# A matmul with GELU: the third product of the opening, evacuated partial sums, a load by row halves and a moved GELU

## Chip, cores, metric

One core of one Trainium2 chip. The metric is the device time of one execution in microseconds (us), the median of several runs.

## The reference

```python
x = np.matmul(a, b)          # a, b: 4096 x 4096 float32
return 0.5 * x * (1 + np.tanh(np.sqrt(2 / np.pi) * (x + 0.044715 * x**3)))
```

## The kernel before

The kernel cuts A, B and the output into quadrants (11, 12, 21, 22) and uses a seven-product scheme (M1 to M7) on them, for 16 groups of 512 rows by 512 columns of each quadrant. Two chains of PSUM banks, X and Y (four banks each, one for each block of 128 rows), take the products. VectorE makes the sums and differences of operands (aS, bS), transposes A and combines results; ScalarE copies PSUM to SBUF and computes GELU; GpSimd issues the loads, which cast f32 to f16.

Group 0 is special, because its operands are still being loaded: the first half of its contraction is done as eight plain products (`PLAIN`), and only the second half by M3, M5, M7, M1, M4, M2, M6, in this order. One step is half a product: 16 matmuls. The parts that matter:

```python
PLAIN = [   # quadrant of C, of A, of B, by row halves
    ("12", "11", "12", False), ("11", "11", "11", False), ("12", "12", "22", False), ("11", "12", "21", False),
    ("21", "21", "11", True), ("21", "22", "21", True), ("22", "21", "12", True), ("22", "22", "22", True),
]
N_WARM = 44
N_IDLE = 10
...
# in settle(), after the last step of a product, for each row block i
elif name == "M7" and not end:
    post["x7", i] = keep("x7", X, RT)          # ScalarE copy, RT = 4 buffers named x7
...
elif name == "M2":
    y = new_y()                                # 5 buffers named y
    tt(y, post.pop(("x1", i)), Y, ALU.subtract)   # VectorE reads bank Y; M6 writes it next
    ...
    waiting.append((gi, i, 1, 0, y, y))
elif name == "M6":
    y = new_y()
    tt(y, Y, post.pop(("x7", i)), ALU.add)
    flush()                                    # adds what is in post, then GELU and output
    ...
...
for n, whats in (      # what is issued ahead of step n; _0 and _1: first and second half
    (0, "A11_0 B12_0 T11_0 B11_0 A12_0 B22_0 B21_0 A21_0"),
    (4, "T12_0 A22_0"), (7, "T21_0"),
    (8, "A11_1+B12_1+B22_1 T22_0 A12_1+B21_1"),
    (14, "T11_1 A22_1 B11_1"), (16, "T12_1 A21_1"), (18, "S2 S3 T22_1"), (22, "T21_1"),
): ...
...
for n, step in enumerate(steps):
    for fn, args in before.get(n, ()):
        fn(*args)
    if n + AHEAD < len(steps):                 # sums are made two steps ahead
        make_sums(*steps[n + AHEAD])           # (cut)
    flush()
    combine()
    plain(n) if step[1] < 0 else multiply(*step)
```

`A` and `B` are loads, `T` is VectorE's transpose of an A block, `S2` and `S3` make M7's B sums ahead of time, `+` mixes loads with one another. Instructions of an engine run in the order in which they are issued here.

Of the kernel before, what the change touches and what calls it, by code (L numbers as in the profile page):

```python
# [8 lines left out]
F16 = mybir.dt.float16  # L9
# [4 lines left out]
ALU = mybir.AluOpType  # L14
AX = mybir.AxisListType

P = 128
Q = 32
NC = 512
# [3 lines left out]
RT = 4  # L23
TM = RT * P
AHEAD = 2
# [16 lines left out]
QPH = 4  # L42
# [1 line left out]


PLAIN = [
    ("12", "11", "12", False), ("11", "11", "11", False), ("12", "12", "22", False), ("11", "12", "21", False),
    ("21", "21", "11", True), ("21", "22", "21", True), ("22", "21", "12", True), ("22", "22", "22", True),
]
N_PLAIN = 2 * len(PLAIN)  # L50
N_WARM = 44
N_IDLE = 10


SQUARE_MAX = 2.0**26
# [45 lines left out]
def half_path(  # L101
# [9 lines left out]
    nc = tc.nc  # L111
    M, K = a.shape
    _, N = b.shape
# [5 lines left out]
    pool = ctx.enter_context(tc.tile_pool(name="sb", bufs=1))  # L119
# [13 lines left out]
    a_tiles, b_tiles = {}, {}  # L133
# [54 lines left out]
    def part(tiles, blk, quad, q):  # L188

        t = tiles[blk, quad, q // 2].rearrange("p x y -> p (x y)")  # L190
        w = 4 * NC
        return t[:, (q % 2) * w : (q % 2 + 1) * w]
# [83 lines left out]
    sums = {}  # L276

    def product(gi, s):
        return (LAST if gi == len(groups) - 1 else PRODUCTS)[s]

    def make_sums(gi, s, q, only=None):
        mb, nb = groups[gi]
        _, _, oa, ob = product(gi, s)
        got = []
        for tiles, blk, o, tag in ((a_tiles, mb, oa, "aS"), (b_tiles, nb, ob, "bS")):
            if only not in (None, tag):
                continue
            if isinstance(o, str):
                got.append(part(tiles, blk, o, q))
                continue  # L290
            if (tag, gi, s, q) in sums:
                got.append(sums.pop((tag, gi, s, q)))
                continue
            t = pool.tile([P, 4 * NC], F16, name=tag, tag=tag, bufs=AHEAD + 1)
            nc.vector.tensor_tensor(  # L295
                out=t[:, :], in0=part(tiles, blk, o[0], q), in1=part(tiles, blk, o[1], q),
                op=ALU.add if o[2] > 0 else ALU.subtract,
            )
            got.append(t)
            if tag == only:  # L300
                sums[tag, gi, s, q] = t
                return
        sums[gi, s, q] = got
# [7 lines left out]
    banks = {}  # L311
    post = {}

    def bank(gi, chain, i):
        par = (gi + (chain == "Y")) % 2
        t = psum_pool.tile([P, NC], F32, name=f"acc{chain}", tag=f"bank{par}{i}")
        banks[chain, i] = t
        return t
# [11 lines left out]
    def warm():  # L330
        z = pool.tile([P, NC], F16, name="zeros", tag="bS", bufs=AHEAD + 1)
        nc.vector.memset(z[:, :], 0.0)
        w = pool.tile([P, P], F16, name="none", tag="none")
        nc.vector.memset(w[:, :], 0.0)
        post["none"] = w
        for i in range(RT):
            bank(0, "X", i)
            bank(0, "Y", i)
        for _ in range(N_WARM):
            nc.tensor.matmul(  # L340
                banks["X", RT - 1][:, :], z[:, :P], z[:, :], start=True, stop=True, skip_group_check=True
            )

    def idle(n):

        for _ in range(n):
            nc.tensor.matmul(
                banks["X", 0][:, :], post["none"][:, :], b_tiles[0, "12", 0][:, 0, :],
                start=False, stop=False, skip_group_check=True,
            )  # L350

    def plain(n):

        (quad, oa, ob, by_rows), h = PLAIN[n // 2], n % 2
        chain = "X" if quad == "11" else "Y"
        seen = [x for x in range(len(PLAIN)) if PLAIN[x][0] == quad]
        sa, sb = a_tiles[0, oa, 0], b_tiles[0, ob, 0]
        sa = sa.rearrange("p jj (m e) -> p jj m e", e=2)
        tiles = [(j, e) for j in range(NJ // 2) for e in range(2) if by_rows or e == h]
        for i in range(h * RT // 2, (h + 1) * RT // 2) if by_rows else range(RT):  # L360
            acc = banks[chain, i]
            start = n // 2 == seen[0] and (by_rows or h == 0)
            stop = n // 2 == seen[-1] and (by_rows or h == 1)
            for j, e in tiles:
                nc.tensor.matmul(
                    acc[:, :], sa[:, j, i * P : (i + 1) * P, e], sb[:, 2 * j + e, :],
                    start=start and (j, e) == tiles[0], stop=stop and (j, e) == tiles[-1],
                    skip_group_check=True,
                )
            if not stop:  # L370
                continue
            if quad == "12":
                post["c12", i] = keep("x7", acc, RT)
            elif quad == "11":
                tt(post["c12", i], post["c12", i], acc, ALU.add)
            elif quad == "21":
                tag = ("energy1", "energy2", "square", "square")[i]
                t = pool.tile([P, W], BF16, name="c21", tag=tag, bufs=1 + (i > 1)).bitcast(F32)
                nc.scalar.copy(out=t[:, :], in_=acc[:, :])
                post["c21", i] = t  # L380
            else:
                tt(post["c12", i], post["c12", i], acc, ALU.subtract)

    def multiply(gi, s, q):
        name, chain = product(gi, s)[:2]
        first = q == 0 and name in ("M3", "M5")
        sa, sb = sums.pop((gi, s, q))
        for i in range(RT):
            acc = bank(gi, chain, i) if first else banks[chain, i]
            products(acc, sa, sb, i, first, q == QPH - 1)  # L390
            if q == QPH - 1:
                settle(gi, name, i)

    def keep(tag, src, bufs):
        t = pool.tile([P, NC], F32, name=tag, tag=tag, bufs=bufs)
        nc.scalar.copy(out=t[:, :], in_=src[:, :])  # L396
        return t
# [3 lines left out]
    def flush():  # L401

        for args in waiting:
            gi, i, ih, jh, y, _ = args
            plain_part = post.pop((f"c{ih + 1}{jh + 1}", i), None) if gi == 0 else None
            if plain_part is not None:
                tt(y, y, plain_part, ALU.add)
            emit(*args)
        waiting.clear()
# [21 lines left out]
    def tt(o, x, y, op):  # L431
        nc.vector.tensor_tensor(out=o[:, :], in0=x[:, :], in1=y[:, :], op=op)  # L432
# [44 lines left out]
    before = {}  # L477
# [5 lines left out]


    for n, whats in (
        (0, "A11_0 B12_0 T11_0 B11_0 A12_0 B22_0 B21_0 A21_0"),
        (4, "T12_0 A22_0"),
        (7, "T21_0"),
        (8, "A11_1+B12_1+B22_1 T22_0 A12_1+B21_1"),
        (14, "T11_1 A22_1 B11_1"),  # L490
        (16, "T12_1 A21_1"),
        (18, "S2 S3 T22_1"),
        (22, "T21_1"),
    ):
        for what in whats.split():
            half = what[-1] == "0" and what != "A11_0"
            if what[0] == "S":
                before.setdefault(n, []).append((make_sums, (0, 2, int(what[1]), "bS")))
                continue
            for h in (0, 1) if half else (None,):  # L500
                args = [(x[0], (0, x[1:3], int(x[4]), h)) for x in what.split("+")]
                if what[0] == "T":
                    before.setdefault(n, []).append((turn_a, args[0][1]))
                else:
                    pairs = [({"A": load_a, "B": load_b}[x], xs) for x, xs in args]
                    before.setdefault(n, []).append((load, pairs))
    before[4].append((idle, (N_IDLE,)))


    nxt_b = {"12": "22", "22": "21", "21": "12", "11": "11"}  # L510
# [33 lines left out]
    for mb in range(NMB):  # L544
        for which, gi in (("b", mb * NNB + 1), ("a", mb * NNB + 2)):
            blk = groups[gi][which == "b"]
# [5 lines left out]
            for x, piece in enumerate(pieces):  # L552
                n = max(x // 2, x - n_two)
# [21 lines left out]
    with tc.manual_schedule():  # L575
        warm()
        table = pool.tile([P, 1], F32, name="table", tag="table")
        nc.vector.memset(table[:, :], 0.0)
        nc.scalar.activation(table[:, :], table[:, :], ACT.Gelu_apprx_tanh)
# [3 lines that stand above are left out]
            if n + AHEAD < len(steps):  # L583
                gi, s, q = steps[n + AHEAD]
                if s >= 0:
                    make_sums(gi, s, q)
            flush()
            combine()
            if step[1] < 0:
                plain(n)  # L590
            else:
                multiply(*step)
        flush()
    return said["value"]

# [35 lines left out]
```

## Time and profile before

| | before |
|---|---|
| time, first three runs | 1581.33 us (1580.16 to 1581.53) |
| span in the profile | 1578.4 us |
| TensorE busy | 99% |
| idle of TensorE after the first real matmul | 2.1 us (0.16, 1.79 and 0.19), and 2.15 us of idle matmuls |

TensorE hardly waits. The real work is 7200 matmuls of 0.216 us; everything in question is in the first 130 us. The prediction shows the lines.

### The profile page before, as it was taken

What the parts mean: (1) busy time and instruction counts of PE and PEld (TensorE: products, weight loads), DVE (VectorE), ACT (ScalarE), POOL (GpSimd) and SP (SyncE); (2) the same over time, 40 slices, a digit from 0 to 9 for tenths busy, and PEclk for the clock granted to TensorE, in tenths of its full rate; (3) what the DMA queues carried; (4) which work ended last, traced back from release to release, by engine and by line L of the source; (5) the groups of instructions that cost most, each with busy time, mean ns of one, the idle gap of its engine ahead of it and who ended that gap; (6) DMA issues with size and microseconds to landing.
All of it is one profiled execution on the core that took longest, in us unless ns stands there. A gap on an engine that the chain in (4) does not pass through costs nothing. (4 is left out here: it accounts for less than half of the span.)

```text
span 1578.4 us, 19668 instructions
## 1 busy us (share of the span) xinstructions
PE 1568.0 (99%) x7254; PEld 710.0 (45%) x7254; DVE 1228.0 (78%) x1371; ACT 517.8 (33%) x710; POOL 537.4 (34%) x976
## 2 busy tenths in 40 slices
PE   9999999999999999999999999999999999999998
PEld 4444444444444444444444444444444444444443
DVE  1498888967787888895778788887687778988775
ACT  0026445311122545531111344542211145364111
POOL 7763442430234144341124414245011443414400
PEclk9999999999999999999999999999999999999999
DMA  9998784892957488586497837779468885747802
GB/s 175 197 225 177 124 170 74 160 168 43 198 104 153 91 133 161 107 174 120 81 164 117 186 73 141 148 110 190 75 120 147 134 160 91 151 106 134 161 27 82
DMA packets 224982, 211.12 MB, mean 134 GB/s; under 512 B 20080, under 2 KB 192112, under 8 KB 224880
## 3 DMA queue, kind: packets, MB, share of 16 engines
q0 software_dynamic: 187584, 142.67, 61.5%
q1 hardware_dynamic: 37296, 67.13, 11.8%
q8 instruction: 59, 0.97, 0.2%
q14 instruction: 43, 0.35, 0.1%
HBM read 285.22 MB, written 67.11 MB: 223 GB/s over the span
## 5 line engine op out<-in xcount | busy, mean ns | idle before, releaser
L325 PEld LDWEIGHTS <-aS 128*128 128x128 f16 x4960 | 485.4, 98 | 587.5 <-issue 2.5
L186 POOL DMA_DIRECT2D bR<-in_b_dram x832 | 449.2, 550 | 702.2 <-DVE bS L295 339.5
L295 DVE TENSOR_TENSOR aS<-aT 128x2048 f16<-128x2048 f16 x310 | 375.9, 1218 | 149.1 <-PE accX L325 112.6
L325 PE MATMUL accX<-bS,aS 128*128 128x512 f16 x1984 | 431.3, 379 | 2.0 <-ACT x L396 1.8
L295 DVE TENSOR_TENSOR bS<-bR 128x2048 f16<-128x2048 f16 x310 | 375.9, 1217 | 69.3 <-PE accX L325 58.5
L325 PEld LDWEIGHTS <-aT 128*128 128x128 f16 x1984 | 194.2, 98 | 234.6 <-issue 0.8
L423 ACT ACTIVATE y<-y 128x512 f32<-128x512 f32 x192 | 118.5, 630 | 353.0 <-DVE y L432 352.7
L325 PE MATMUL accY<-bS,aT 128*128 128x512 f16 x992 | 216.9, 379 | 0.2 <-DVE bS L295 0.2
L325 PE MATMUL accX<-bR,aS 128*128 128x512 f16 x992 | 216.7, 379 | 0.0
L325 PE MATMUL accY<-bR,aS 128*128 128x512 f16 x992 | 216.7, 379 | 0.0
L325 PE MATMUL accX<-bS,aT 128*128 128x512 f16 x992 | 216.7, 379 | 0.0
L325 PE MATMUL accY<-bS,aS 128*128 128x512 f16 x992 | 216.7, 379 | 0.0
L186 POOL DMA_DIRECT2D stage<-in_a_dram x140 | 88.1, 635 | 247.6 <-DVE aT L161 177.6
L432 DVE TENSOR_TENSOR energy<-energy,square 128x1024 bf16<-128x1024 bf16 x240 | 164.4, 685 | 9.6 <-ACT square L207 5.7
L396 ACT COPY x<-accX 128x512 f32<-128x512 f32 x128 | 74.8, 587 | 223.5 <-PE accX L325 223.5
L207 ACT ACTIVATE square<-aT 128x1024 bf16<-128x1024 f16 x120 | 123.4, 1051 | 70.4 <-DVE energy L432 70.1
L207 ACT ACTIVATE square<-bR 128x1024 bf16<-128x1024 f16 x120 | 123.0, 1051 | 62.4 <-DVE energy L432 61.1
L161 DVE STREAM_TRANSPOSE aT<-stage 128x2048 uint32<-128x2048 uint32 (+1 forms) x36 | 74.4, 2068 | 62.5 <-DMA stage<-in_a_dram 49.0
L396 ACT COPY m<-accX 128x512 f32<-128x512 f32 x60 | 34.8, 580 | 194.3 <-PE accX L325 192.0
L423 ACT ACTIVATE y<-accX 128x512 f32<-128x512 f32 x64 | 38.2, 597 | 100.1 <-PE accX L325 99.9
L432 DVE TENSOR_TENSOR x<-accX,x 128x512 f32<-128x512 f32 x64 | 44.0, 691 | 21.8 <-ACT y L423 19.1
L432 DVE TENSOR_TENSOR y<-accY,m 128x512 f32<-128x512 f32 x60 | 39.9, 687 | 12.5 <-ACT m L396 12.4
(40 smaller groups left out, 340.2 us busy)
## 6 DMA issues: line engine op xcount, KB each, us to landing
bR<-in_b_dram POOLq DMA_DIRECT2D x832, 128.0 KB, 5.3
out_dram<-y SPq DMA_DIRECT2D x256, 256.0 KB, 5.7
stage<-in_a_dram POOLq DMA_DIRECT2D x116, 256.0 KB, 6.9
stage<-in_a_dram POOLq DMA_DIRECT2D x24, 128.0 KB, 5.1
row<-seen_d SPq DMA_DIRECT2D x2, 1.5 KB, 3.9
seen_d<-seen SPq DMA_DIRECT2D x1, 3.0 KB, 7.0
```

The costliest lines, as they stand in the source:

```text
L161: nc.vector.transpose(dst[:, :, x, :], src[:, :, x, :])
L186: nc.gpsimd.dma_start(out=dst, in_=src)
L207: nc.scalar.activation(t[:, :], src, ACT.Square)
L295: nc.vector.tensor_tensor(out=t[:, :], in0=part(tiles, blk, o[0], q), in1=part(tiles, blk, o[1], q), op=ALU.add if o[2] > 0 else ALU.subtract,
L325: nc.tensor.matmul(acc[:, :], sa[:, j // 2, i * P : (i + 1) * P, j % 2], sb[:, j, :], start=start and j == 0, stop=stop and j == 3, skip_g ...
L396: nc.scalar.copy(out=t[:, :], in_=src[:, :])
L423: nc.scalar.activation(y[:, :], src[:, :], ACT.Gelu_apprx_tanh)
L432: nc.vector.tensor_tensor(out=o[:, :], in0=x[:, :], in1=y[:, :], op=op)
```

## The change

The intent is to take the two idle stretches of TensorE out of the opening. A21's product comes third, when only A21 has to be loaded for it, so that no idle matmuls are needed there; C12 and C21 are therefore taken out of PSUM after their first product and completed by additions. A22 of the second half is loaded, transposed and summed by row halves, so that M7 can start on the first. The GELU of C12 is moved behind M7's copies, which M1 waits for. The call that is moved, `flush()`, also holds VectorE's additions of C12's parts, so these move too.

```diff
 PLAIN = [
-    ("12", "11", "12", False), ("11", "11", "11", False), ("12", "12", "22", False), ("11", "12", "21", False),
-    ("21", "21", "11", True), ("21", "22", "21", True), ("22", "21", "12", True), ("22", "22", "22", True),
+    ("12", "11", "12", False), ("11", "11", "11", False), ("21", "21", "11", True),
+    ("12", "12", "22", False), ("11", "12", "21", False), ("21", "22", "21", True),
+    ("22", "21", "12", True), ("22", "22", "22", True),
 ]
-N_WARM = 44
-N_IDLE = 10
+N_WARM = 46
... (make_sums takes a row half h)
... (idle() and its call go)
+            if not kept and n // 2 == seen[1]:
+                tt(post[c, i], post[c, i], acc, ALU.add)
-            if quad == "12":
-                post["c12", i] = keep("x7", acc, RT)
+            elif quad == "12":
+                post[c, i] = keep("x7", acc, RT)
...
-        (0, "A11_0 B12_0 T11_0 B11_0 A12_0 B22_0 B21_0 A21_0"),
-        (4, "T12_0 A22_0"),
-        (7, "T21_0"),
-        (8, "A11_1+B12_1+B22_1 T22_0 A12_1+B21_1"),
+        (0, "A11_0 B12_0 T11_0 B11_0 A21_0 A12_0 B22_0 B21_0"),
+        (4, "T21_0 A22_0"),
+        (6, "T12_0"),
+        (8, "A11_1+B12_1+B22_1"),
+        (9, "T22_0 A12_1+B21_1"),
... (T21_1 from step 22 to 23; A22_1 and T22_1 by halves, each followed by its half sums)
-            flush()
+            if step[:2] != (0, 2):
+                flush()
             combine()
...
+            if step == (0, 2, QPH - 1):
+                flush()
```

More of the change, by code (lines that the diff above doesn't have):

```diff
@@ L279, in product, with make_sums @@
         return (LAST if gi == len(groups) - 1 else PRODUCTS)[s]
-    def make_sums(gi, s, q, only=None):
+    def make_sums(gi, s, q, only=None, h=None):
         mb, nb = groups[gi]
@@ L290, in make_sums @@
                 continue
-            if (tag, gi, s, q) in sums:
-                got.append(sums.pop((tag, gi, s, q)))
-                continue
-            t = pool.tile([P, 4 * NC], F16, name=tag, tag=tag, bufs=AHEAD + 1)
-            nc.vector.tensor_tensor(
-                out=t[:, :], in0=part(tiles, blk, o[0], q), in1=part(tiles, blk, o[1], q),
-                op=ALU.add if o[2] > 0 else ALU.subtract,
-            )
+            t = sums.pop((tag, gi, s, q), None)
+            if t is None or h:
+                if t is None:
+                    t = pool.tile([P, 4 * NC], F16, name=tag, tag=tag, bufs=AHEAD + 1)
+                x, y, z = t[:, :], part(tiles, blk, o[0], q), part(tiles, blk, o[1], q)
+                if h is not None:
+                    x, y, z = (
+                        v.rearrange("p (jj m) -> p jj m", jj=2)[:, :, h * TM : (h + 1) * TM]
+                        for v in (x, y, z)
+                    )
+                nc.vector.tensor_tensor(
+                    out=x, in0=y, in1=z, op=ALU.add if o[2] > 0 else ALU.subtract
+                )
             got.append(t)
@@ L332, in warm @@
         nc.vector.memset(z[:, :], 0.0)
-        w = pool.tile([P, P], F16, name="none", tag="none")
-        nc.vector.memset(w[:, :], 0.0)
-        post["none"] = w
         for i in range(RT):
@@ L341, in warm @@
                 banks["X", RT - 1][:, :], z[:, :P], z[:, :], start=True, stop=True, skip_group_check=True
-            )
-    def idle(n):
-        for _ in range(n):
-            nc.tensor.matmul(
-                banks["X", 0][:, :], post["none"][:, :], b_tiles[0, "12", 0][:, 0, :],
-                start=False, stop=False, skip_group_check=True,
             )
@@ L361, in plain @@
             acc = banks[chain, i]
-            start = n // 2 == seen[0] and (by_rows or h == 0)
-            stop = n // 2 == seen[-1] and (by_rows or h == 1)
+            kept = quad in ("11", "22")
+            start = (n // 2 == seen[0] or not kept) and (by_rows or h == 0)
+            stop = (n // 2 == seen[-1] or not kept) and (by_rows or h == 1)
+            c = f"c{quad}"
             for j, e in tiles:
@@ L379, in plain @@
                 nc.scalar.copy(out=t[:, :], in_=acc[:, :])
-                post["c21", i] = t
+                post[c, i] = t
             else:
@@ L492, in half_path @@
         (18, "S2 S3 T22_1"),
-        (22, "T21_1"),
+        (23, "T21_1"),
     ):
         for what in whats.split():
-            half = what[-1] == "0" and what != "A11_0"
+            half = what[-1] == "0" and what != "A11_0" or what in ("A22_1", "T22_1")
             if what[0] == "S":
@@ L503, in half_path @@
                     before.setdefault(n, []).append((turn_a, args[0][1]))
+                    if what == "T22_1":
+                        for q in range(QPH // 2, QPH):
+                            before[n].append((make_sums, (0, 2, q, "aS", h)))
                 else:
@@ L506, in half_path @@
                     before.setdefault(n, []).append((load, pairs))
-    before[4].append((idle, (N_IDLE,)))
     nxt_b = {"12": "22", "22": "21", "21": "12", "11": "11"}
```

## The prediction

> **What bounds the kernel now.** I read the page first. TensorE is busy 99% of the span, so only its idle time and its extra matmuls can be won back, and the timeline of TensorE tells where those are (columns: start, length, engine, line, what; in brackets the idle time before and who ended it):
>
> ```profile
> PE 1568.0 (99%) x7254; PEld 710.0 (45%) x7254; DVE 1228.0 (78%) x1371; ACT 517.8 (33%) x710; POOL 537.4 (34%) x976
> ...
> 1.42 11.08 PE L340 MATMUL accX<-zeros 128*128 128x512 f16 x44 [1.42 <-DVE zeros L332]
> 14.12 7.07 PE L365 MATMUL accY<-bR,aT 128*128 128x512 f16 x32 [1.61 <-DMA bR<-in_b_dram]
> ...
> 27.93 2.32 PE L347 MATMUL accX<-bR,none 128*128 128x512 f16 x10
> 30.08 7.07 PE L365 MATMUL accY<-bR,aT 128*128 128x512 f16 x32
> ...
> 71.52 7.07 PE L325 MATMUL accY<-bS,aT 128*128 128x512 f16 x32
> 78.43 7.07 PE L325 MATMUL accX<-bR,aS 128*128 128x512 f16 x32
> 85.34 1.89 PE L325 MATMUL accX<-bS,aS 128*128 128x512 f16 x8
> 87.39 5.34 PE L325 MATMUL accX<-bS,aS 128*128 128x512 f16 x24 [0.16 <-ACT m L396]
> 94.52 7.07 PE L325 MATMUL accX<-bS,aS 128*128 128x512 f16 x32 [1.79 <-ACT x L396]
> ...
> 115.24 7.07 PE L325 MATMUL accY<-bS,aS 128*128 128x512 f16 x32
> ```
>
> A product of 32 matmuls takes 6.91 us from start to start (21.02 less 14.12, 101.42 less 94.52). After the first real matmul at 14.12 TensorE loses 2.15 us to the ten idle matmuls (30.08 less 27.93), 0.16 and 1.79 to ScalarE's copies, and 0.19 at 129.40 in group 1. From there to the end at 1578.4 the table of waits shows TensorE no other wait. So the most that the change can win is 4.3 us, 0.27%.
>
> Then I asked what would stand behind TensorE if it were earlier. First the windows (busy us of each engine in a stretch, then clock, share of DMA, GB/s written):
>
> ```profile
> 60.00:65.00 5.00, 5.00 (x25) 2.23 (x23) 1.62 (x1) 0.00 (x0) 3.78 (x8) 1.00 1.33 198
> 65.00:70.00 5.00, 5.00 (x24) 2.24 (x23) 4.13 (x5) 0.00 (x0) 3.05 (x6) 1.00 1.34 199
> ...
> 90.00:100.00 10.00, 8.21 (x39) 3.68 (x38) 10.00 (x11) 5.06 (x10) 6.40 (x12) 1.00 1.20 245
> 100.00:110.00 10.00, 10.00 (x48) 4.50 (x47) 9.86 (x16) 4.05 (x7) 7.04 (x13) 1.00 1.23 213
> ```
>
> Up to 75 us the loads write a steady 190 to 200 GB/s. Read one by one in the trace, the landings come every 0.65 us for 128 KB from 11.4 to 74.4 us, without a hole: the opening is a full stream of loads. From 80 us on VectorE is the full one. Its own timeline shows where that begins and ends:
>
> ```profile
> 74.46 2.31 DVE L161 STREAM_TRANSPOSE aT<-stage 128x2048 uint32<-128x2048 uint32 x1 [2.05 <-DMA stage<-in_a_dram]
> 76.81 2.36 DVE L295 TENSOR_TENSOR aS<-aT 128x2048 f16<-128x2048 f16 x2
> 79.08 2.35 DVE L295 TENSOR_TENSOR bS<-bR 128x2048 f16<-128x2048 f16 x2
> 81.35 2.30 DVE L161 STREAM_TRANSPOSE aT<-stage 128x2048 uint32<-128x2048 uint32 x1
> 83.69 2.36 DVE L295 TENSOR_TENSOR aS<-aT 128x2048 f16<-128x2048 f16 x2
> 85.97 2.69 DVE L432 TENSOR_TENSOR y<-accY,m 128x512 f32<-128x512 f32 x4
> ...
> 114.48 2.47 DVE L432 TENSOR_TENSOR y<-x,accY 128x512 f32<-128x512 f32 x4
> ```
>
> At 74.46 VectorE begins the transpose of A12's second half, the moment that A12 has landed. From there to 114.48 its instructions stand end to end. At 114.48 it reads the Y banks for M2's result, and M6 may write bank Y of row block 0 only after that: the first read ends at 115.16, M6 begins at 115.24. TensorE shows no wait there, but the margin is 0.08 us.
>
> **What the Trainium skill says.** (1) "VectorE: DVE Perf Modes", the perf-mode tier table, has tensor_tensor of 2048 elements at 1224 ns for two-byte data in SBUF and one element a cycle for fp32 or PSUM; the trace agrees: 1217 ns on the page for the f16 sums, 687 ns for 512 elements from PSUM. (2) The same page, on the errata, says that each instruction pays a fixed extra; the trace shows it: a transpose of half size takes 1.20 to 1.25 us against 2.31, so halving costs a little. (3) "TensorE: Matmul & The Clock Gate", the table of goals, warns of TensorE gaps over about 3 us; gaps of 1.61 and 1.79 here left the pace at 6.91 us a product and the granted clock at 1.00. My gaps below stay under 2.5 us, so I charge no clock. (4) "DMA: Bandwidth & Descriptors", issuing engines are not separate queues: all loads share the 16 engines. The landings agree: they form one row, and only order can be changed.
>
> **The change part by part.** *Opening.* The first real matmul is set by B12's landing (13.98) and A11's transpose (13.9): it stays at 14.12; two more warm matmuls only shorten the gap before it. Two products reach 27.93 as before. Third comes A21 times B11, by row halves, with A21 in A12's old place in the stream: the transposes end at 25.86 and 28.6, needed at 27.93 and 31.4. No wait, so the ten idle matmuls go: minus 2.15. The fourth needs half of B22, sixth megabyte of the stream; before, the load in that place was half landed at 35.02, and TensorE arrives at 34.84: plus 0.3 or 0.4. After that each product has its data: A22's first half lands at 45.8 and is needed at 49. The evacuation added (four ScalarE copies move earlier, eight VectorE additions of 0.69 us) falls where VectorE is idle (51 to 63 us) or in the other chain's product. So the plain products end at about 69.8 in place of 71.52, and M3 starts 1.75 us earlier: its operands are there at 66.8.
>
> *M5.* It needs A11 less A12 of the second half. The bytes ahead of A12's last transfer are the same 12.9 MB in both orders, so it lands at 74.4 again: transpose 2.31, sum 1.14, ready at 78.0. TensorE would arrive at 76.7 and waits 1.4. M5 starts at 78.1 against 78.43: of 1.75, 0.35 is left.
>
> *A22 by row halves.* VectorE does two half transposes (2 x 1.26) and four half sums (4 x 0.60, an estimate from the 0.60 us pitch of other instructions with the same number of cycles) for 81.35 to 85.97, 4.62 us: 4.92, that is plus 0.3. M7 can start at 85.0 with the first row half, but the third row block waits for ScalarE's copy of M5, which waits for a buffer that VectorE frees in its first y after the sums: about 86.3 plus 0.7 plus 0.6 gives 87.6 where TensorE arrives at 86.7. A wait of 0.8; M7 ends at 92.7, as before.
>
> *GELU of C12 behind the copies.* In the kernel before, the x copies stand behind four GELUs that wait for VectorE (first copy 93.90). Now they follow M7 directly, so the 1.79 goes and M1 starts at 92.7 against 94.52: 1.8 us earlier. M4 and M2 keep that (sums ready at 97.3 and 101.9 for 99.6 and 106.5).
>
> *M6.* VectorE's row from 74.46 to the first read for M2 holds the same instructions in another order, plus the 0.3: the additions of C12 come after M1's sums in place of before, A21's transpose one sum later, but all before it. So that read ends at 115.16 + 0.3 = 115.5, where TensorE would arrive at 113.4. It waits 2.1 us, and M6 starts at 115.5 against 115.24. All that was won is given back here, and 0.3 more. The 0.19 in group 1 hangs on the same VectorE row and moves along.
>
> Sum from 14.12 to M6: minus 2.15 idle matmuls, minus 0.16 and minus 1.79 ScalarE waits, plus 0.35 (B22), 1.4 (A12), 0.8 (buffer of M5's copy), 2.0 (M2's read): plus 0.4 from these rounded terms, plus 0.3 by the direct count of VectorE's row, which I trust more. 1581.33 + 0.3 is 1581.6; since a different order may save some of the row's small holes I take 1581.4.
>
> **The rivals.** (a) *All of it is won*: the waits at M5 and M6 don't appear and the time is 1577.5. For it: TensorE's list of waits shows only what the change removes. Against it: the landing at 74.38 and a VectorE row 40 us long without holes. Chance 8%. (b) *Part is won*: the stream delivers A12 a microsecond earlier, and the whole VectorE row moves with it: 1580. For it: the first megabyte took until 11.4, though later ones take 5.3 us each. Against it: nothing in the change touches the first loads. 17%. (c) *VectorE gets slower*: half sums with strided rows lose the two-byte rate (four times about 1.14 in place of 0.60, an estimate from the full-size sums), plus 2.2 us on the row: 1583.8. Against it: each run of a half is still 512 contiguous elements. 10%. (d) *The reordered waits cool the clock*: a few us more. Gaps too short; 3%. The rest is the sum above.
>
> **Range and chances.** The runs before spread over 1580.16 to 1581.53, so 0.7 us of noise to either side. With (b) mostly inside and (a) and (c) outside, 1579.4 to 1583.0 should hold it 8 times in 10. Two per cent is 32 us: no path here has that size, neither way.
>
> **What would show it right or wrong.** In the timeline of the changed kernel: third product at 27.9 without idle matmuls; a wait for B22 before the fourth at about 35; M3 near 69.8; M5 near 78.1 after 1.4 us, put down to VectorE's sum; a wait within M7; M1 near 92.7 without a wait for the x copies; VectorE without a hole from 74.5 on; M6 at 115.5 after some 2 us for VectorE's y. If M6 starts by 114 the row was shorter than I count and the prediction is too high; if A12's transpose starts before 73.5 it is rival (b); half sums over 0.9 us are rival (c).

## The result

| | before | after |
|---|---|---|
| median of 6 runs | 1580.41 us (1579.75 to 1581.53) | 1580.47 us (1580.01 to 1581.59) |
| span in the profile | 1578.4 us | 1579.0 us |
| matmuls | 7254 | 7246 |

The ratio is 1.0, 95% interval 0.9988 to 1.0013: the same. TensorE's timeline of the changed kernel (columns as in the prediction; source lines have moved a little):

```profile
13.07 7.07 PE L362 MATMUL accY<-bR,aT 128*128 128x512 f16 x32 [0.18 <-DMA bR<-in_b_dram]
...
26.88 7.07 PE L362 MATMUL accY<-bR,aT 128*128 128x512 f16 x32
34.89 7.07 PE L362 MATMUL accY<-bR,aT 128*128 128x512 f16 x32 [0.94 <-DMA bR<-in_b_dram]
...
69.42 7.07 PE L331 MATMUL accY<-bS,aT 128*128 128x512 f16 x32
77.77 7.08 PE L331 MATMUL accX<-bR,aS 128*128 128x512 f16 x32 [1.28 <-DVE aS L302]
84.69 0.59 PE L331 MATMUL accX<-bS,aS 128*128 128x512 f16 x2
85.66 1.47 PE L331 MATMUL accX<-bS,aS 128*128 128x512 f16 x6 [0.38 <-DVE aS L302]
87.54 5.34 PE L331 MATMUL accX<-bS,aS 128*128 128x512 f16 x24 [0.41 <-ACT m L395]
94.68 7.07 PE L331 MATMUL accX<-bS,aS 128*128 128x512 f16 x32 [1.80 <-ACT x L395]
...
115.39 7.07 PE L331 MATMUL accY<-bS,aS 128*128 128x512 f16 x32
...
129.66 7.07 PE L331 MATMUL accY<-bS,aT 128*128 128x512 f16 x32 [0.28 <-DVE bS L302]
```

The idle matmuls are gone and M3 starts 2.1 us earlier (69.42 against 71.52); half of that is the first real matmul, which started 1.05 us earlier in this execution. Then the lead melts: 1.28 before M5, 0.79 within M7. The 1.80 before M1, which was to go, is still there, and M1 and M6 start within 0.16 us of where they did before (94.52 and 115.24). VectorE's timeline shows what they wait for:

```profile
74.14 2.31 DVE L161 STREAM_TRANSPOSE aT<-stage 128x2048 uint32<-128x2048 uint32 x1 [3.83 <-DMA stage<-in_a_dram]
...
81.04 1.24 DVE L161 STREAM_TRANSPOSE aT<-stage 128x1024 uint32<-128x1024 uint32 x1
82.31 1.29 DVE L302 TENSOR_TENSOR aS<-aT 128x1024 f16<-128x1024 f16 x2
83.64 1.25 DVE L161 STREAM_TRANSPOSE aT<-stage 128x1024 uint32<-128x1024 uint32 x1
84.92 1.29 DVE L302 TENSOR_TENSOR aS<-aT 128x1024 f16<-128x1024 f16 x2
86.13 2.68 DVE L431 TENSOR_TENSOR y<-accY,m 128x512 f32<-128x512 f32 x4
...
93.27 2.49 DVE L431 TENSOR_TENSOR y<-y,x 128x512 f32<-128x512 f32 x4
...
114.64 2.48 DVE L431 TENSOR_TENSOR y<-x,accY 128x512 f32<-128x512 f32 x4
```

This row of instructions, one directly behind the other, begins again when A12 lands and runs without a hole to M2's read at 114.64. ScalarE's timelines, first before, then after, show the copies ahead of M1:

```profile
91.56 2.43 ACT L423 ACTIVATE y<-y 128x512 f32<-128x512 f32 x4 [3.63 <-DVE y L432]
93.90 2.03 ACT L396 COPY x<-accX 128x512 f32<-128x512 f32 x4
```

```profile
94.04 2.39 ACT L395 COPY x<-accX 128x512 f32<-128x512 f32 x4 [5.96 <-DVE y L431]
96.33 2.19 ACT L422 ACTIVATE y<-y 128x512 f32<-128x512 f32 x4
```

The order is changed as intended, but the first copy does not start earlier. It waits for VectorE's addition at 93.27, because the parts of C12 lie in the four buffers named x7 that the copies of M7 need; a buffer is free only when its part has been added. In the kernel before, the same additions stood earlier on VectorE, ahead of M1's second pair of sums; `flush()` took them along:

```profile
90.84 2.49 DVE L432 TENSOR_TENSOR y<-y,x 128x512 f32<-128x512 f32 x4
```

A measure will be used below that the noise of the loads does not touch, as long as no later load makes a hole in the row: M6's start less the start of A12's transpose. It is 40.78 us before and 41.25 after.

### The profile page after: what moved, and what is told of

The parts are those of the page before. It is cut to its first block, busy times and chain, and to the rows that moved or that the text cites. A ratio compares the mean times of both kernels' runs of the same rounds, so it can differ in the third digit from the quotient of the medians.

```text
span 1579.0 us, 19681 instructions
## 1 busy us (share of the span) xinstructions
PE 1566.6 (99%) x7246; PEld 709.1 (45%) x7246; DVE 1233.6 (78%) x1381; ACT 517.7 (33%) x710; POOL 537.6 (34%) x980
## 3 DMA queue, kind: packets, MB, share of 16 engines
q1 hardware_dynamic: 37296, 67.13, 11.8%
## 5 line engine op out<-in xcount | busy, mean ns | idle before, releaser
L302 DVE TENSOR_TENSOR aS<-aT 128x2048 f16<-128x2048 f16 (+1 forms) x312 | 376.3, 1212 | 150.2 <-PE accX L331 113.8
```

Of the source, the lines that this page charges most:

```text
L302: nc.vector.tensor_tensor(out=x, in0=y, in1=z, op=ALU.add if o[2] > 0 else ALU.subtract)
```

## The experiments

Theory: VectorE's unbroken row, from the landing of A12's second half to M2's read, sets the time. What the change wins ahead of that row is waited away inside it, at whichever wait comes last. Main rivals: the x7 buffers alone; the idle matmuls really cost 2.15 us and something unrelated ate the gain; the order of loads alone.

The twelve runs came in three jobs, each on another chip, five rounds each. The kernel before, beside them: 1579.70, 1580.28 and 1580.48 us (nine runs each). Of the twelve ratios to it only that of `both` has an interval clear of 1. For the others the argument rests on the traces, one execution each.

### The idle matmuls alone

```diff
-    before[4].append((idle, (N_IDLE,)))     # in the kernel before
```

> The kernel before, without its ten idle matmuls, nothing else. Theory: the third product waits for half of B22 in their place (it starts at about 29.9 in place of 30.1, 0.2 us earlier at most), M5, M1 and M6 start as before, time unchanged within 0.5 us of 1580.4. Rival (the idle matmuls cost their 2.15 us): 1578.3.

1579.91 us, ratio 1.0003 (0.9989 to 1.0017): unchanged. TensorE's timeline of this kernel:

```profile
29.73 7.07 PE L365 MATMUL accY<-bR,aT 128*128 128x512 f16 x32 [2.09 <-DMA bR<-in_b_dram]
```

In place of the idle matmuls stands a wait of 2.09 us for B22. They had filled a hole; taking them out was worth nothing by itself.

### C12 in other buffers

```diff
-                post[c, i] = keep("x7", acc, RT)
+                post[c, i] = keep("x1", acc, RT)    # the changed kernel; x1 is free until M1 ends
```

> The changed kernel, with the evacuated parts of C12 in the buffers of x1 in place of those of x7, so that M7's copies need not wait for the additions of C12. Theory (VectorE's row from the landing of A12 to M2's read sets the time of M6): the wait of 1.80 us before M1 goes, M1 starts at about 92.9 in place of 94.68, but M6 still starts at about 115.4, now after a wait of 1.7 us for VectorE's y; time unchanged, within 0.7 us of the changed kernel's 1580.5. Rival (the buffer of x7 is what keeps the gain back): M6 starts at 113.6 and the time falls by 1.8 us to 1578.7.

> The kernel of c12_in_x1 once more, because its times (median 1582.4) lay 2 us above the theory's 1580.5, while in its trace only the first loads were late (first matmul at 14.57, A12's transpose at 75.9 in place of 74.1) and M6 stood 41.22 us after that transpose as in the changed kernel (41.25). If that was chance in the loads: median within 0.8 us of 1580.5, M6 41.2 us after the transpose. If the other buffers for C12 cost something: again 1582 or more.

First 1582.41 us, ratio 1.0014 (1.0000 to 1.0027), then 1581.93, ratio 1.0003 (0.9990 to 1.0017). TensorE's timeline of the second:

```profile
87.75 12.25 PE L331 MATMUL accX<-bS,aS 128*128 128x512 f16 x56 [0.41 <-ACT m L395]
...
115.57 7.07 PE L331 MATMUL accY<-bS,aS 128*128 128x512 f16 x32 [1.76 <-DVE y L431]
```

M7 and M1 now run through (56 matmuls without a break), so the buffers did hold the copies. But M6 then waits 1.76 us for M2's read, and starts 41.22 us after A12's transpose in both runs: nothing is won. That is the wait that the prediction had at this place. The times of the first run lie above what was expected, and in its trace the loads were late from the start (A11 landed at 11.83 us, 10.33 in the changed kernel's). Two of the five times of the repeat were 1580.0 and 1580.1, three about 1582. Whether these buffers make late loads more likely, or it was chance, stays open; the next kernel has the same buffers and a median of 1580.41 us.

### The same buffers, GELU at its old place

```diff
-            if step[:2] != (0, 2):
-                flush()
+            flush()
...
-            if step == (0, 2, QPH - 1):
-                flush()
```

> The changed kernel with C12 in x1's buffers but the GELU of C12 at its old place, ahead of M7's copies. Theory (two things hold these copies, the buffers and ScalarE's order, and each alone suffices): M1 again 20.5 us after A12's transpose as in the changed kernel (94.68 less 74.14), not 18.6 as in c12_in_x1; M6 at 41.2, time as the changed kernel. Rival (the buffers alone held them): M1 at 18.6 us.

1580.41 us, ratio 0.9998 (0.9984 to 1.0012). M1 starts 20.53 us after A12's transpose, as in the changed kernel (20.54), and M6 41.24 us after it. So either of two things is enough to hold M7's copies: ScalarE's order, as here, or the x7 buffers when the additions come late, as in the changed kernel. The change removed the first and, by moving the additions with the GELU, brought in the second. Moving the GELU alone was not tested. An estimate from this run: its additions start 16.85 us after the transpose, which is 91.0 by the changed kernel's clock; with 0.69 for the first addition and 0.59 for the first copy that copy would end at 92.3, before M1's 92.7. Then the x7 buffers would not have held M1, and only M2's read would have held M6.

### One sum twice

```diff
-                nc.vector.tensor_tensor(
+                for _ in range(2 if (gi, s, q) == (0, 5, 2) else 1):
+                    nc.vector.tensor_tensor(
... (the arguments are the same)
```

> The changed kernel, with the first of the two A sums of M2 made twice in the same buffer (1.13 us more on VectorE, after M1's copies and before M2's read; result unchanged). Theory (VectorE's row sets M6, with no slack in it): M2's read ends 1.13 us later, a wait of 1.1 us for VectorE's y appears before M6, and all after it is 1.1 us later, so about 1581.6 against the changed kernel's 1580.5. Rival (only the x7 buffer before M1 binds, the row behind it has slack): no wait before M6, time as the changed kernel. Read from the trace as M6's start less the start of A12's transpose: 41.25 us in the changed kernel, 42.4 by the theory.

1582.38 us, ratio 1.0011 (0.9998 to 1.0025), which is 0.8 us more than expected and 1.9 us over the changed kernel's first median. The interval still holds 1, so the time alone shows nothing. TensorE's timeline:

```profile
118.03 7.07 PE L332 MATMUL accY<-bS,aS 128*128 128x512 f16 x32 [1.08 <-DVE y L432]
```

The wait appears, 1.08 us. M6 stands 42.66 us after A12's transpose, 1.41 more than in the changed kernel, where 1.13 was expected; A12 itself landed 1.2 us later here. The other 0.3 us lie in two places of VectorE's timeline: two of A22's half sums took 1.47 us in place of 1.29, and the doubled sum lengthened the row by 1.26. The row has no slack, as the theory has it.

### A22 whole again

```diff
-            half = what[-1] == "0" and what != "A11_0" or what in ("A22_1", "T22_1")
+            half = what[-1] == "0" and what != "A11_0"
```

> The changed kernel without its halving of A22 of the second half: one transpose and whole sums, as before. Theory: VectorE's row is shorter by the 0.47 us that the halves cost (5.09 less 4.62 us from the transpose to the y of M5), M6's start less the start of A12's transpose is 40.8 us in place of 41.25, time 0.4 to 0.5 us less. Rival (halving lets M7 start earlier, and that counts): M1 and M6 later, time 0.4 us or more above the changed kernel.

1580.74 us, ratio 0.9998 (0.9985 to 1.0012). M6 comes 40.78 us after the transpose: the halves cost 0.47 us, to the hundredth what the row of before had less. In the times the expected gain of 0.4 to 0.5 us does not show: the five runs spread over 1579.66 to 1581.51, and in the traced one A12's transpose started at 74.78 in place of 74.14. The early start for M7 was not there either: in the changed kernel's timeline above, only two of M7's matmuls run on the first half before the third waits for a later half sum (0.38 us). By the code the third matmul reads rows of the first half too, so it is not data that it waits for; why the wait was set is not shown.

### A12 ahead of B21: the start of the row

```diff
-        (9, "T22_0 A12_1+B21_1"),
+        (9, "T22_0 A12_1 B21_1"),
```

> The changed kernel, with the loads of A12's second half in front of those of B21 in place of mixed with them; same bytes. Theory: A12 lands at about 70 in place of 74.1, its transpose starts at about 70.3, M5 does not wait (1.28 us gone), and VectorE's row, held then by B21's landing at 74.8, stands 3.4 us earlier at the y of M5 (82.8 in place of 86.1) and at M2's read (111.2 in place of 114.6); M6 starts at about 112.0 in place of 115.4 and the time falls by about 3.2 us to 1577.3. Rival (the x7 buffer or the clock or noise set the time, not the row's start): M5's wait goes but M6 starts at 115 or so, time within 0.7 us of 1580.5.

> The kernel before, with the same new order of A12 and B21. Theory: M5 was bound by TensorE at 78.43, so M5 stays; the row is earlier by about 1 us only (A22's landing at 80.4 holds it); M1 starts at 93.6 in place of 94.5, M6 at 114.3, time 0.9 us less: 1579.5. So the change would be worth about 2.3 us with this order, and nothing without. Rival (the order alone is worth the whole gain and the new opening nothing): 1577.3, the same as the changed kernel with this order.

On the changed kernel: 1578.32 us, ratio 0.9989 (0.9975 to 1.0002), about 1.7 us less by the means (1577.3 was expected; the interval holds 1); M5 does not wait and M6 starts at 112.58. That is 2.8 us earlier than in the changed kernel, 3.4 expected: the row starts 3.6 us earlier, at 70.52, but loses 0.8 before the y of M5 at 83.32, in part to a wait of 0.22 for A22. Then 1 us goes again in group 1, as these lines of TensorE and of VectorE show:

```profile
127.79 7.07 PE L331 MATMUL accY<-bS,aT 128*128 128x512 f16 x32 [1.24 <-DVE bS L302]
```

```profile
122.98 0.69 DVE L431 TENSOR_TENSOR y<-accY,x 128x512 f32<-128x512 f32 x1 [3.40 <-DMA out_dram<-y]
...
126.53 1.22 DVE L302 TENSOR_TENSOR bS<-bR 128x2048 f16<-128x2048 f16 x1
```

M6's results need y buffers that M2's output transfers still hold; VectorE waits for them with group 1's sums behind it in its queue. I had not counted this as a second end of the row.

On the kernel before: 1579.48 us, ratio 0.9997 (0.9984 to 1.0011), 0.2 us less by the medians where 0.9 was expected. Its row starts earlier, at 72.86, but then has a hole:

```profile
81.51 2.31 DVE L161 STREAM_TRANSPOSE aT<-stage 128x2048 uint32<-128x2048 uint32 x1 [1.67 <-DMA stage<-in_a_dram]
```

It waits for A22, which landed 1 us later in this run than in that of before, and M6 starts at 115.39. The stream of loads was already 1.0 us late where the new order begins (65.46 against 64.45), so the order is not what made A22 late. So neither the new opening nor the new order of loads gives a clear gain alone. The intervals of the two kernels with the new order overlap, and the difference between them rests on the traces.

### The end of the row

Three edits to the changed kernel: C12 in x1's buffers as above; M2's reads before the second pair of M6's sums; M6's result in place in x7's buffer in group 0. `reads_first` is the same without the third.

```diff
+            read_first = step == (0, 5, QPH - 1)
-            if n + AHEAD < len(steps):
+            if n + AHEAD < len(steps) and not read_first:
 ...
                 multiply(*step)
+            if read_first:
+                make_sums(*steps[n + AHEAD])
 ...
-            y = new_y()
-            tt(y, Y, post.pop(("x7", i)), ALU.add)
+            x7 = post.pop(("x7", i))
+            y = new_y() if gi else x7
+            tt(y, Y, x7, ALU.add)
```

> The changed kernel with the end of VectorE's row released: parts of C12 in x1's buffers, M2's four reads before M6's second pair of sums in place of after, and M6's result made in place in x7's buffer, so that it waits for no output transfer. No instruction less. Theory: M1 at 92.9 and M6 at 113.6 (in place of 94.7 and 115.4, with A12's transpose at 74.1), no wait before M6, none before the second half of group 1's M3: 2.2 us less from A12's landing to group 1, time about 1578.2. Rival (something else holds M6 or M3, for example the loads of group 1): a wait of 1 to 2 us comes back in group 1 and the time is within 0.7 us of 1580.5.

> row_end without its third part: M6's result in new y buffers as before. Theory: M6 still 39.3 us after A12's transpose, as in row_end, but VectorE then waits for the output transfers of M2's result, so the second half of group 1's M3 starts 55.5 us after A12's transpose as in the changed kernel (129.66 less 74.14), in place of 53.4; the gain of 1.9 us is given back there and the time is that of the changed kernel. Rival (reading first is enough): 53.4 us, time as row_end, 1578.6.

`reads_first`: 1580.16 us, ratio 0.9999 (0.9985 to 1.0012). M6 comes 39.29 us after the transpose, as predicted, and the gain is given back where it was said to be:

```profile
113.39 7.33 PE L331 MATMUL accY<-bS,aS 128*128 128x512 f16 x32
120.56 7.07 PE L331 MATMUL accY<-bS,aT 128*128 128x512 f16 x32
129.53 7.07 PE L331 MATMUL accY<-bS,aT 128*128 128x512 f16 x32 [1.90 <-DVE bS L302]
```

129.53 less the transpose's 74.09 is 55.44 us; in the changed kernel 129.66 less 74.14 is 55.52. `row_end`: 1578.65 us, ratio 0.9991 (0.9977 to 1.0004); M6 at 39.30 us, and group 1's M3 runs its 64 matmuls without a break. The same gain of the row, kept, because nothing behind it waits any more: the only edit between the two runs is where M6's result is put. In the time it is within the noise.

### Both ends

This is `row_end` with the loads of `a12_first`.

> The same, and A12's second half loaded before B21: both ends of VectorE's row released. Theory: M5 without a wait, M1 at 90.3, M6 at 111.0, the second half of group 1's M3 at 124.8 in place of 129.7 (first matmul at 13.1); time 4.8 us below the changed kernel, about 1575.3. Rival (the two gains are one and the same): no better than with A12 first alone, 1578.3.

1575.48 us (1575.32 to 1576.32) against 1580.28 beside it, ratio 0.9968 (0.9954 to 0.9982), close to the 1575.3 expected. This is 0.3% less than the kernel before, which is clear of the noise; the changed kernel did not run in the same job. TensorE's timeline from M5 on has no wait left:

```profile
76.16 7.07 PE L331 MATMUL accX<-bR,aS 128*128 128x512 f16 x32
83.06 13.98 PE L331 MATMUL accX<-bS,aS 128*128 128x512 f16 x64
...
117.59 13.98 PE L331 MATMUL accY<-bS,aT 128*128 128x512 f16 x64
```

### The changed kernel again

> The changed kernel itself once more, beside the kernel before on the same chip. Theory: ratio within 0.05% of 1, M6 41.2 us after the start of A12's transpose wherever that falls.

1580.01 us (1579.89 to 1584.62, four of the five within 0.6 us), ratio 1.0001 (0.9988 to 1.0015), M6 again 41.25 us after the transpose, which started at 73.92.

## Why the prediction was right, point by point

- **Time.** 1581.4 predicted, 1580.47 measured, within the range; no gain, as said. The prediction counted from 1581.33, the median of the first three runs; over six runs the kernel before has 1580.41. So the 0.9 us lie in that base. The change itself was put at plus 0.1 to 0.3 us and measured at plus 0.06, which the noise does not tell apart.
- **Opening.** Right in kind: third product without idle matmuls, then a wait for B22. That wait was 0.94, not 0.35: the first loads happened to land about 1.05 us earlier in this run (first matmul at 13.07), B22's half only 0.26 (34.76 for 35.02), and TensorE waited longer there. M3 at 69.4 (69.8 predicted). That more warm matmuls only shorten the gap before the first real one did not hold in every run: in seven of the eleven traces with 46 of them the first real matmul followed them without a wait, in `row_end` at 14.24 although its part of B12 had landed at 13.40.
- **M5.** Right: 1.28 us of wait (1.4 predicted), start 3.63 us after A12's transpose (74.46 to 78.1 predicted, 3.6).
- **M7.** 0.38 + 0.41 = 0.79 us of waits, 0.8 predicted. But half of it was for the half sums, which I had taken to cost TensorE nothing. The cost of the halves on VectorE was mis-sized: 0.47 us, not 0.3 (two half sums take 1.29 us, and each change between transpose and sum has a small gap).
- **M1: this step was wrong.** "Now they follow M7 directly, so the 1.79 goes and M1 starts at 92.7." It stayed, at 1.80. I had looked at ScalarE's order and not at where C12's parts lie: the copies needed their buffers. I had even written that the additions of C12 come after M1's sums now, but not that this keeps the buffers longer. The runs with x1's buffers show the start that I predicted (18.58 us after the transpose, 92.7 by the changed kernel's clock).
- **M6: the wait was not where I put it.** I predicted 2.1 us before M6; there is none, because the 1.80 before M1 took its place. With the buffers moved it appears, 1.76 us. The start is right all the same, 115.39 for 115.5, because both waits hang on one row of VectorE. That the two bounds meet was luck: after the addition at 93.27 TensorE's way through M1, M4 and M2 and VectorE's way to M2's read happen to take the same time (M6 41.25 us after the transpose when the first binds, 41.22 when the second does). A longer hold at M1 would have made the prediction too low. The bound by the row itself held.
- **Loads as one stream.** The landings form one row, as said. But GpSimd issues all the loads here, so no run tests what the page says of several issuing engines.
- **Rivals.** All is won (a): no. Slow half sums (c): no, two take 1.29 us. A cooled clock (d): no, the clock stayed at 0.999 to 1.0. Part is won (b): the transpose started 0.3 us earlier, and the halves took that back.

## What to carry to other kernels

When a wait of the busy engine is removed, ask which unbroken row of another engine stands behind it, when that row can start and which of its instructions the busy engine needs; the gain counts only if the row starts earlier, gets shorter or is asked for less. Here all gains in front of VectorE's row came to nothing, and 0.3% came when a load was moved so that the row starts earlier and what TensorE and the output transfers ask of it at its end was released. For a buffer that a copy waits for, check both the queue order and who held the buffer last, and what else moves with the instructions that you move. Whether the new opening is needed for the 0.3% was not tested: the two edits of `both` were not made to the kernel before. And where the loads vary from run to run, measure from a landing, not from the start of the program.

## What the Trainium skill lacked or had wrong

- "VectorE: DVE Perf Modes", the errata table: it gives 58 + FD/Accel cycles for SBUF to SBUF and 120 + FD/Accel for PSUM to SBUF (FD: elements in a row, Accel: 2 for these f16 sums, 1 for f32). From start to start in an unbroken row, the first fits: 1.135 us measured for f16 sums of 2048 elements (four in the changed kernel from 110.10 to 114.64), 1.127 by an estimate from the page. The second is too high here: an estimate from it is 0.66 us for 512 elements, and four f32 sums that read PSUM take 2.39 us (114.64 to 117.03), 0.60 each. Four f32 sums from SBUF alone take as long (118.16 to 120.57).
- No page says how uncertain the first loads are: over the fourteen traces the first megabyte landed between 9.9 and 11.8 us. That spread is nearly what the change was meant to win at its largest place (2.15 us).
- "Perfetto Trace Analysis", Optimization Strategy: it advises to find the gaps of the most contended engine and what blocks them, and to make those dependencies start sooner or complete faster. Here two gaps so found were taken away without effect on M6 (the idle matmuls' 2.15 us in `no_idle`, the 1.80 us before M1 in `c12_in_x1`). It lacks the next step: to follow the blocking engine's own unbroken row to its start, and to check the place 41 us later where it is needed again.
